# Attention keys projected ahead of values, values handled by halves, and stepped reads in place of stepped writes

## The chip, the cores and the metric

The kernel runs on one core of one Trainium2 chip. Five engines work at the same time, each through its own list of instructions in order: PE multiplies matrices, DVE (the vector engine) and ACT (the scalar engine) work on tiles, POOL does vector work and starts DMAs, SP starts DMAs. Engines wait for each other through semaphores. The metric is the time on the device in microseconds (us), lower is better. A tile lies in SBUF; the results of PE lie in PSUM.

## What is computed

One layer of a decoder trunk over 1024 tokens with 1024 channels, in float32. The input is normalised and projected; three groups of heads mix the tokens; their outputs are joined, projected and added to the stream; a gated MLP with a short convolution and a gated per-layer embedding follow, and a last normalisation.

```python
z = rmsnorm(h, norm_mix_g[l]) @ w_in[l]
a_q, a_f, a_i, a_g, b_q, b_k, b_v, c_in = jnp.split(z, splits, axis=-1)
o_a = hgrn2_mix(a_q, a_f, a_i, a_g, lbs[l], hgrn_gnorm_g[l])
o_b = dilated_window_mix(b_q, b_k, b_v)
o_c, v_first = rwkv7_mix(c_in, ...)
h = h + jnp.concatenate([o_a, o_b.astype(o_a.dtype), o_c.astype(o_a.dtype)], axis=-1) @ w_out[l]
h = h + conv_glu_ffn(rmsnorm(h, norm_ffn_g[l]), ffn_up[l], ffn_conv_w[l], ffn_conv_b[l], ffn_down[l])
gate = jax.nn.sigmoid(rmsnorm(h, norm_ple_g[l]) @ ple_gate[l])
h = h + gate * (p[l] @ ple_proj[l])
return rmsnorm(h, final_norm_g)
```

The change lies in `dilated_window_mix` and in what feeds it. That is a causal attention of four heads of 64 channels, in which each token looks back through three windows at once: the last 128 tokens, the last 512 in steps of 4, and the last 2048 in steps of 16. The first is called near here and the other two far. Tokens whose numbers have the same rest by 4 are a class; the far windows stay within a class.

## The kernel before

**Products in three passes.** Float32 operands are split in a high and a low half, and every large product is made of three matmuls (`mm3`, lines L154, L156, L158). The weight's high half is a cast on ACT (L126). The low half is made in one of two ways that alternate with a running number, `self.uid`: a subtraction on DVE (L132), or a negative copy on ACT and a POOL DMA that adds the weight again (L129, L130).

**Stages.** First the RWKV heads (`rwkv`), with the first projections running beside them as filling. Then `phase_mix` runs five streams in turn, by a list written by hand: `A` and `B` the HGRN heads (`hgrn_head`, two after each other in each stream), `C` the windowed attention (`swa`), `F` the last four projections (`project_late`), `M` what is left of the filling. The lists of the engines follow the order in which these streams issue. Then comes the output projection (L1638 stands on its matmuls and on those of the MLP), the MLP and the embedding.

**Projections into DRAM.** Each of the projected groups of 128 channels, numbered j, goes through a tile `zst` (L556 multiplies by the norm's factor `rstd`) to a DRAM tensor `z`, and is loaded again as `zl` where it is needed (`zload`, L591). Groups 24 to 29 are queries, keys and values of the attention: 24, 25, 26 for the first pair of heads (p=0), 27, 28, 29 for the second (p=1). For these `by_class` turns the two views of L556, so that the tokens of each block of 128 lie by class in `zst`. Groups 24 to 27 are finished in one operation of 128x1024 (source `dp`), 28 and 29 in two halves of 128x512 (source `zp`), each with its own store (L579). The list `js` sets the order of the projections; its last four, here 29, 28, 18, 22, are those of stream `F`.

**The attention.** `swa` runs over the pairs p and, in each, ten steps `qb`. `swa_load` starts the loads of q, k and v on POOL's queue (for p=1 in step 7 of p=0). `swa_values_in` turns v with eight transposes (`vt`, L1267), copies them to `sV` on ACT (L1268), and SP writes them to a DRAM tensor `vd` in four DMAs (L1272). In step 2 `swa_far_values` reads all of `vd` back as `sW` in one DMA (L1276). A step makes scores (`swq`, L1296 near and L1304 far), a masked copy with a running minimum on DVE (`lg`, L1318), the exponential on ACT (L1319), transposes (`swt`, L1335), near values (`swo`, L1350) and, every fourth step, far values (`swf`, L1360, added by L1364). `swa_out` then spreads the reciprocal sums over the channels with 16 matmuls (`swd`, L223) and multiplies (L1373), once for the blocks 0 to 3 and once for the blocks 4 to 7 of a pair, in the step after their far values.

**Beside it** in the rows below: `hsc` (L1121) are scores of an HGRN head, masked on DVE into `hS` (L1123 to L1128); `qt` (L1134) and `hk` (L1132) scale its queries and keys from level to level; L1075 makes `qt` from a loaded q; `hss`, `hrs` and `ho` (L1198, L1201 on POOL, L1203) are its norm; L1405 splits a finished head for the output projection. `Tb` and `Tt` (L783, L785) are the RWKV inverse, a chain of small operations on DVE, whose result goes through two DMAs (`Tz`, `Tc`) to `py` (L896).

Of the kernel before, what the change touches and what calls it, by code (L numbers as in the profile page):

```python
# [10 lines left out]
F32 = mybir.dt.float32  # L11
# [3 lines left out]
ALU = mybir.AluOpType  # L15
# [3 lines left out]
P = 128  # L19
T = 1024  # L20
HT = 512
ND = 8
# [69 lines left out]
class Trunk:  # L92
# [197 lines left out]
    def slot(self, s):  # L290
        return self.slots.tile([P, T], F32, tag="slot", name=self.nm(s), bufs=self.NSLOT)
# [257 lines left out]
    def by_class(self, j, dst, *src):  # L549
        if j < 24:  # L550
            return dst, *src
        return dst.rearrange("p (b c i) -> p b i c", c=4, i=32), *(t.rearrange("p (b i c) -> p b i c", c=4, i=32) for t in src)

    def finish(self, kind, dst, src, r):
        if kind == 2:
# [53 lines left out]
    def rwkv(self):  # L609
        nc, tc = self.nc, self.tc  # L610
        lt = self.mix_in(0, 6, "lora")
        nc.scalar.activation(lt[0:64, :], lt[0:64, :], AF.Tanh)
        sg = self.mix_in(1, 7, "sg")
        nc.scalar.activation(sg, sg, AF.Sigmoid)
        self.z, self.quiet = {}, False
        js = iter((*range(8, 16), 24, 25, 26, 16, 17, 20, 21, 19, 23, 27, 29, 28, 18, 22))
        for p in (0, 1):
            d = {}
            lead, n = self.FILL[p]
            fill = self.project_rest([next(js) for _ in range(n)])  # L620
            with tc.tile_pool(name=f"pre{p}", bufs=1) as tp:
                self.rwkv_prep(p, tp, lt, d, fill)
                self.rwkv_inverse(p, tp, d)
            for i in range(8 * lead - (3 if p else 8)):
                self.quiet = i >= 8 * lead - 20
                next(fill)
                if p == 0 and i == 1:
                    d["v"] = self.mix_in(4, 4, "v")
                if i == (7 if p else 16):
                    self.rwkv_bonus(d)  # L630
            with tc.tile_pool(name=f"rk{p}", bufs=1) as rp:
                self.quiet = False
                self.rwkv_main(p, rp, sg, d, fill)
            self.rwkv_norm(p, sg, d, 1, fill, 6 - 3 * p)
            if p == 0:
                for _ in fill:
                    pass
        self.rest, self.more = list(js), fill
# [259 lines left out]
    def rwkv_group(self, g, rp, d):  # L898
# [9 lines left out]
        def c3(t):  # L908
            return t.rearrange("p (c i) -> p c i", i=64)[:, cs, :]
# [14 lines left out]
        be, kh, v = c3(d["be"]), c3(d["kh"]), c3(d["v"])  # L924
        W, KV = rt("W", [P, 2, 4, 128], 3), rt("KV", [P, 2, 4, 64], 3)
        for srcs, dst in (((a, be), W[:, :, :, 0:64]), ((kh, v), KV)):
            pt = mx("pt", 2, 4, 64)
# [132 lines left out]
    def hgrn_head(self, h):  # L1060
# [52 lines left out]
        for l in range(1, 8):  # L1113
# [30 lines left out]
            yield  # L1144
        V = self.slot("hV")
        for hf in (0, 1):
            pt = mxp.tile([P, HT], F32, tag="mx", name=self.nm("vt"))
            for c in range(4):
                nc.tensor.transpose(pt[:, c * P:(c + 1) * P], vc[:, hf * HT + c * P:hf * HT + (c + 1) * P], self.ident)
            nc.scalar.copy(V[:, hf * HT:(hf + 1) * HT], pt)  # L1150
        kt = self.slot("hkt")
# [12 lines left out]
        for hf in (0, 1):  # L1164
            pk = mxp.tile([P, 4, P], F32, tag="mx", name=self.nm("hkv"))
            for c in range(4):
                cc = hf * 4 + c
                if cc == 7:
                    break
                nc.tensor.matmul(pk[:, c, :], kt[:, at(cc, True)], V[:, at(cc)], start=True, stop=True)  # L1170
            for c in range(4):
# [12 lines left out]
        for hf in (0, 1):  # L1184
            po = mxp.tile([P, 4, P], F32, tag="mx", name=self.nm("hpo"))
            for c in range(4):
                cc = 7 - c if hf == 0 else c
                s = at(cc)
                nc.tensor.matmul(po[:, c, :], S[:, s], V[:, s], start=True, stop=cc == 0)
                if cc:  # L1190
# [36 lines left out]
    def swa(self, sp):  # L1227

        pend, fin, load = [], None, self.swa_load(sp, 0)
        self.nc.gpsimd.dma_start(self.swmask, self.a["swm"])  # L1230
        yield
        for p in (0, 1):
            d = load
            self.swa_values_in(d)
            for qb in range(10):
                if fin:
                    self.swa_out(*fin)
                    fin = None
                if qb == 2:
                    self.swa_far_values(d)  # L1240
                if qb < 8:
                    cur = self.swa_scores(sp, d, qb)
                if qb > 1:
                    fin = self.swa_values(sp, d, *pend.pop(0))
                if 0 < qb < 9:
                    pend[-1:] = [self.swa_turn(sp, *pend[-1])]
                if qb < 8:
                    pend.append((qb, *cur))
                if qb == 7 and p == 0:
                    load = self.swa_load(sp, 1)  # L1250
                yield
        self.swa_out(*fin)

    def swa_load(self, sp, p):
        d = {"p": p}
        for i, n in enumerate("qkv"):
            d[n] = self.zload(24 + 3 * p + i, lambda n: sp.tile([P, T], F32, tag="sslot", name=self.nm(n), bufs=5),
                              self.nc.gpsimd)
        return d

    def swa_values_in(self, d):
        nc, vc = self.nc, d["v"]
        V = self.sp.tile([P, T], F32, tag="sslot", name=self.nm("sV"), bufs=5)
        for hf in (0, 1):
            pt = self.mxp.tile([P, HT], F32, tag="mx", name=self.nm("vt"))
            for c in range(4):
                nc.tensor.transpose(pt[:, c * P:(c + 1) * P], vc[:, hf * HT + c * P:hf * HT + (c + 1) * P], self.ident)  # L1267
            nc.scalar.copy(V[:, hf * HT:(hf + 1) * HT], pt)  # L1268
        d["V"] = V.rearrange("p (b c) -> p b c", c=P)
        d["vd"] = vd = self.zpool.tile([4, ND, 32, P], F32, tag=f"vd{d['p']}", name=f"vd{d['p']}")  # L1270
        for c in range(4):
            nc.sync.dma_start(vd[c].rearrange("b i x -> i b x"), d["V"][32 * c:32 * c + 32])  # L1272

    def swa_far_values(self, d):
        W = self.sp.tile([P, ND, P], F32, tag="sslot", name=self.nm("sW"), bufs=5)
        self.nc.sync.dma_start(W, d["vd"].rearrange("c (g b) i x -> (b i) (c g) x", g=2))  # L1276
        d["W"] = W

    HEADS = slice(0, 64), slice(64, 128)

# [59 lines left out]
    def swa_values(self, sp, d, qb, den, pT):  # L1340
        nc, near = self.nc, pT[0]
        if qb == 0:
            d["o"] = self.sp.tile([P, T], F32, tag="sslot", name=self.nm("ob"), bufs=5) if d["p"] else                 self.keep.tile([P, T], F32, tag="zst", name=self.nm("ob"), bufs=2)
        o = d["o"]
        po = self.mxp.tile([P, P], F32, tag="mx", name=self.nm("swo"))

        blocks = range(max(qb - 1, 0), qb + 1)
        for i, kb in enumerate(blocks):
            for h, hs in enumerate(self.HEADS):
                self.mark = nc.tensor.matmul(po[hs, :], d["V"][:, kb, hs], near[h][:, i * P:(i + 1) * P],  # L1350
                                             start=i == 0, stop=kb == qb).ins
        nc.scalar.copy(o[:, qb * P:(qb + 1) * P].rearrange("p (i c) -> p i c", c=4), po.rearrange("p (c i) -> p i c", c=4))
        if qb % 4 == 3:
            nc.vector.reciprocal(den[:, :8], den[:, :8])
            pf = self.mxp.tile([P, 4, P], F32, tag="mx", name=self.nm("swf"))
            for c in range(4):
                cs = slice(32 * c, 32 * c + 32)
                for g in range(1 + qb // 4):
                    for h, hs in enumerate(self.HEADS):
                        self.mark = nc.tensor.matmul(pf[hs, :, cs], d["W"][:, 2 * c + g, hs],  # L1360
                                                     pT[1][h][:, :, g * P + 32 * c:g * P + 32 * c + 32],
                                                     start=g == 0, stop=g == qb // 4).ins
            on = o[:, (qb - 3) * P:(qb + 1) * P].rearrange("p (b i c) -> p b i c", c=4, i=32)
            nc.vector.tensor_tensor(on, on, pf.rearrange("p b (c i) -> p b i c", c=4), ALU.add)  # L1364
            return d, qb, o, den

    def swa_out(self, d, qb, o, den):
        nc, k = self.nc, 4 + d["p"]
        pd = self.mxp.tile([P, HT], F32, tag="mx", name=self.nm("swd"))
        self.spread2(pd, den, 4)  # L1370
        os = slice((qb - 3) * P, (qb + 1) * P)
        nat = "p (b i c) -> p b i c"
        nc.vector.tensor_tensor(self.final(k, qb == 3, o[:, os]).rearrange(nat, c=4, i=32), o[:, os].rearrange(nat, c=4, i=32),  # L1373
                                pd.rearrange("p (b c i) -> p b i c", c=4, i=32), ALU.mult)
        if qb == 7:
            self.o[k] = o
            self.o_done(k)
# [819 lines left out]
```

## Time and profile before

| | us |
|---|---|
| median of three timed runs | 1393.27 (1393.27 to 1393.94) |
| the profiled execution's own time | 1394.56 |
| span of its instructions | 1392.8 |
| PE busy | 1356.2 (97%) |
| DVE busy | 1059.5 (76%) |
| ACT busy | 648.4 (47%) |
| POOL busy | 350.7 (25%) |

The profile is of one execution. Its times count from the start of the span; the granted clock of PE is given as a share of full speed. In the rows of the timeline the columns are start, duration, engine, line, operation, the tile written and the tiles read, their shapes and the count, and in brackets how long the engine was idle before and what ended that. A start, a plus and a duration give an end. Since matmuls overlap, the time that a group takes from PE is the distance from its start to the next group's start.

### The profile page before, as it was taken

What the parts mean: (1) busy time and instruction counts of PE and PEld (TensorE: products, weight loads), DVE (VectorE), ACT (ScalarE), POOL (GpSimd) and SP (SyncE); (2) the same over time, 40 slices, a digit from 0 to 9 for tenths busy, and PEclk for the clock granted to TensorE, in tenths of its full rate; (3) what the DMA queues carried; (4) which work ended last, traced back from release to release, by engine and by line L of the source; (5) the groups of instructions that cost most, each with busy time, mean ns of one, the idle gap of its engine ahead of it and who ended that gap; (6) DMA issues with size and microseconds to landing.
All of it is one profiled execution on the core that took longest, in us unless ns stands there. A gap on an engine that the chain in (4) does not pass through costs nothing.

```text
span 1392.8 us, 22767 instructions
## 1 busy us (share of the span) xinstructions
PE 1356.2 (97%) x8717; PEld 1101.8 (79%) x8717; DVE 1059.5 (76%) x1689; ACT 648.4 (47%) x1139; POOL 350.7 (25%) x288
## 2 busy tenths in 40 slices
PE   9999999999998999998999999999999999999997
PEld 7878777877876877787888888888888888888886
DVE  7585456835666797789798898888898799677665
ACT  7633433234354464575644434344434445455662
POOL 0211122101321121221254445454543000002321
PEclk9999999999998999999999999999999999999998
DMA  6355533645942311895433233222225963442674
GB/s 233 84 143 146 137 108 91 173 89 142 287 140 99 93 61 62 230 303 177 136 107 106 100 112 113 86 102 101 99 99 190 340 218 106 128 138 68 174 205 136
DMA packets 101757, 197.12 MB, mean 142 GB/s; under 512 B 22160, under 2 KB 28560, under 8 KB 101648
## 3 DMA queue, kind: packets, MB, share of 16 engines
q1 hardware_dynamic: 77040, 157.54, 33.5%
q0 software_dynamic: 13536, 26.86, 10.6%
q10 hardware_dynamic: 11072, 11.28, 2.4%
q8 instruction: 68, 1.11, 0.3%
q14 instruction: 41, 0.34, 0.1%
HBM read 142.42 MB, written 51.64 MB: 139 GB/s over the span
## 4 chain that ended last, share of the span: by engine, by line
PE 84%; DVE 8%; ACT 3%; DMA 2%; issue 1%; POOL 1%; SPq 0%; DVEq 0%; ACTq 0%; POOLq 0%
PE bg L1638 17%; PE bv L1638 13%; PE bv L1965 7%; PE bg L1965 7%; PE dp L154 5%; PE dp L156 5%; PE dp L158 5%; PE dp L1638 3%; PE zo L1638 2%; PE bv L154 1%; PE bv L158 1%; PE bv L156 1%; PE bg L154 1%; PE bg L158 1%; PE bg L156 1%
## 5 line engine op out<-in xcount | busy, mean ns | idle before, releaser
L132 POOL TENSOR_TENSOR wlo<-raw,whi 128x512 fp32r<-128x512 f32 x80 | 128.3, 1622 | 69.7 <-ACT whi L126 69.7
L1638 PE MATMUL bg<-t,whi 128*128 128x512 f32 x352 | 135.0, 395 | 4.6 <-DVE h L1664 4.6
L126 ACT CAST whi<-wraw 128x512 fp32r<-128x512 f32 x120 | 73.6, 618 | 138.6 <-PE dp L156 97.3
L154 PE MATMUL dp<-xh,whi 128*128 128x512 f32 x416 | 136.2, 408 | 0.9 <-DVE r L605 0.8
L158 PE MATMUL dp<-xh,wlo 128*128 128x512 f32 x416 | 130.0, 392 | 0.0
L156 PE MATMUL dp<-xl,whi 128*128 128x512 f32 x416 | 129.3, 391 | 0.1
L126 ACT CAST whi<-raw 128x512 fp32r<-128x512 f32 x88 | 52.4, 620 | 97.7 <-issue 51.2
L1965 PE MATMUL bg<-t,whi 128*128 128x512 f32 x308 | 95.2, 390 | 0.0
L1965 PE MATMUL bv<-t,whi 128*128 128x512 f32 x308 | 94.9, 389 | 0.0
L158 PEld LDWEIGHTS dp<-xh,wlo 128*128 128x128 f32 x416 | 77.9, 188 | 19.2 <-issue 2.0
L156 PEld LDWEIGHTS dp<-xl,whi 128*128 128x128 f32 x416 | 78.2, 188 | 17.4 <-DVE xl L428 0.5
L126 ACT CAST whi<-s 128x512 fp32r<-128x512 f32 x65 | 38.5, 620 | 112.9 <-PE bg L1638 111.0
L132 POOL TENSOR_TENSOR wlo<-s,whi 128x512 fp32r<-128x512 f32 x40 | 59.0, 1475 | 126.1 <-ACT whi L126 126.1
L154 PEld LDWEIGHTS dp<-xh,whi 128*128 128x128 f32 x416 | 74.7, 188 | 20.2 <-issue 5.1
L1638 PEld LDWEIGHTS bg<-t,whi 128*128 128x128 f32 x352 | 67.0, 191 | 19.1 <-DVE h L1664 5.0
L130 POOL DMA_DIRECT2D wlo<-in_w_in_dram x27 | 24.0, 913 | 187.3 <-ACT wlo L129 149.0
L209 POOL TENSOR_TENSOR rst<-rst,mhalf 128x4 f32<-128x4 f32 (+2 forms) x8 | 9.7, 1218 | 243.0 <-DVE rst L205 228.5
L1961 ACT CAST t<-t 128x512 fp32r<-128x512 f32 x77 | 47.8, 622 | 45.6 <-PE bv L1965 32.3
L1638 PE MATMUL bg<-t,wlo 128*128 128x512 f32 x176 | 68.8, 395 | 0.0
L1965 PEld LDWEIGHTS bv<-t,whi 128*128 128x128 f32 x308 | 57.8, 188 | 12.0
L1965 PEld LDWEIGHTS bg<-t,whi 128*128 128x128 f32 x308 | 57.8, 188 | 11.9
L132 DVE TENSOR_TENSOR wlo<-wraw,whi 128x512 fp32r<-128x512 f32 x77 | 52.5, 684 | 18.8 <-ACT whi L126 16.3
(480 smaller groups left out, 3675.7 us busy)
## 6 DMA issues: line engine op xcount, KB each, us to landing
raw<-in_ffn_up_dram SPq DMA_DIRECT2D x44, 512.0 KB, 3.3
wraw<-in_w_in_dram SPq DMA_DIRECT2D x27, 512.0 KB, 4.2
z<-zst SPq DMA_DIRECT2D x18, 512.0 KB, 3.1
gb<-ct SPq DMA_DIRECT2D x33, 256.0 KB, 2.3
t<-gb SPq DMA_DIRECT2D x33, 256.0 KB, 2.7
t<-gt SPq DMA_DIRECT2D x33, 256.0 KB, 2.6
zl<-z SPq DMA_DIRECT2D x16, 512.0 KB, 4.8
wraw<-in_ple_gate_dram SPq DMA_DIRECT2D x16, 512.0 KB, 4.1
```

Source lines behind the costliest of these rows:

```text
L126: self.cast = nc.scalar.copy(hi, src).ins
L130: nc.gpsimd.dma_start(lo, eng, accum_op=ALU.add)
L132: eng.tensor_tensor(lo, src, hi.bitcast(F32), ALU.subtract)
L154: nc.tensor.matmul(ps[hf], wh, xh[hf], start=first, stop=False)
L156: nc.tensor.matmul(ps[hf], wh, xl[hf], start=False, stop=False)
L158: self.step = nc.tensor.matmul(ps[hf], wl, xh[hf], start=False, stop=last).ins
L209: self.pow = nc.gpsimd.tensor_tensor(r2, r, self.mhalf[:, :n], ALU.pow).ins
L1638: self.step = nc.tensor.matmul(ps, w[part == 2][:, s], X[k][part == 1], start=start and k == part == 0, stop=k == 3 and part == 2, skip_gr ...
L1961: nc.scalar.copy(xh, x)
L1965: nc.tensor.matmul(ps[m], wt[part == 2][:, m * P:(m + 1) * P], (xh, xl)[part == 1], start=k == part == 0, stop=k == NK - 1 and part == 2)
```

## The change

It has four parts. First, `by_class` writes `zst` in order and reads `dp`, `zp` and `rstd` in steps of four, where before it read in order and wrote in steps; the contents of `zst` stay the same. Second, the late keys (28) are projected ahead of the late values (29). Third, v comes in two halves: two loads of 256 KB, four transposes and one copy for each, the second half in step 2; `vd` is written in eight DMAs of 64 KB, and `sW` read in two of 256 KB, in steps 2 and 5. Fourth, the last `swa_out` (p=1, blocks 4 to 7) spreads and multiplies in four PSUM tiles of 128 columns.

```diff
     def by_class(self, j, dst, *src):
         if j < 24:
             return dst, *src
-        return dst.rearrange("p (b c i) -> p b i c", c=4, i=32), *(t.rearrange("p (b i c) -> p b i c", c=4, i=32) for t in src)
+        return dst.rearrange("p (b c i) -> p b c i", c=4, i=32), *(t.rearrange("p (b i c) -> p b c i", c=4, i=32) for t in src)
...
-        js = iter((*range(8, 16), 24, 25, 26, 16, 17, 20, 21, 19, 23, 27, 29, 28, 18, 22))
+        js = iter((*range(8, 16), 24, 25, 26, 16, 17, 20, 21, 19, 23, 27, 28, 29, 18, 22))
...
-            self.swa_values_in(d)
+            self.swa_values_in(d, 0)
             for qb in range(10):
...
-                if qb == 2:
-                    self.swa_far_values(d)
+                if qb in (2, 5):
+                    self.swa_far_values(d, qb // 5)
...
+                if qb == 0:
+                    self.swa_load_v(d, 1)
+                if qb == 2:
+                    self.swa_values_in(d, 1)
                 if qb == 7 and p == 0:
                     load = self.swa_load(sp, 1)
...
     def swa_load(self, sp, p):
-        d = {"p": p}
-        for i, n in enumerate("qkv"):
-            d[n] = self.zload(24 + 3 * p + i, lambda n: sp.tile([P, T], F32, tag="sslot", name=self.nm(n), bufs=5),
-                              self.nc.gpsimd)
+        d = {"p": p, "W": {}}
+        slot = lambda n: sp.tile([P, T], F32, tag="sslot", name=self.nm(n), bufs=5)
+        for i, n in enumerate("qk"):
+            d[n] = self.zload(24 + 3 * p + i, slot, self.nc.gpsimd)
+        d["v"], d["V"] = slot("v"), None
+        self.swa_load_v(d, 0)
         return d
...
+    def swa_load_v(self, d, g):
+        gs = slice(g * HT, (g + 1) * HT)
+        self.nc.gpsimd.dma_start(d["v"][:, gs], self.z[26 + 3 * d["p"]][:, gs])
...
+    def swa_values_in(self, d, g):
+        nc = self.nc
+        if g == 0:
+            V = self.sp.tile([P, T], F32, tag="sslot", name=self.nm("sV"), bufs=5)
+            d["V"] = V.rearrange("p (b c) -> p b c", c=P)
+            d["vd"] = self.zpool.tile([2, 4, 4, 32, P], F32, tag=f"vd{d['p']}", name=f"vd{d['p']}")
+        pt = self.mxp.tile([P, 4, P], F32, tag="mx", name=self.nm("vt"))
+        for b in range(4):
+            o = g * HT + b * P
+            nc.tensor.transpose(pt[:, b], d["v"][:, o:o + P], self.ident)
+        V = d["V"][:, 4 * g:4 * g + 4]
+        nc.scalar.copy(V, pt)
         for c in range(4):
-            nc.sync.dma_start(vd[c].rearrange("b i x -> i b x"), d["V"][32 * c:32 * c + 32])
-
-    def swa_far_values(self, d):
-        W = self.sp.tile([P, ND, P], F32, tag="sslot", name=self.nm("sW"), bufs=5)
-        self.nc.sync.dma_start(W, d["vd"].rearrange("c (g b) i x -> (b i) (c g) x", g=2))
-        d["W"] = W
+            nc.sync.dma_start(d["vd"][g, c].rearrange("b i x -> i b x"), V[32 * c:32 * c + 32])
+
+    def swa_far_values(self, d, g):
+        if g == 0:
+            d["W"] = self.sp.tile([P, 2, 4, P], F32, tag="sslot", name=self.nm("sW"), bufs=5)
+        self.nc.sync.dma_start(d["W"][:, g], d["vd"][g].rearrange("c b i x -> (b i) c x"))
...
     def swa_out(self, d, qb, o, den):
         nc, k = self.nc, 4 + d["p"]
-        pd = self.mxp.tile([P, HT], F32, tag="mx", name=self.nm("swd"))
-        self.spread2(pd, den, 4)
         os = slice((qb - 3) * P, (qb + 1) * P)
         nat = "p (b i c) -> p b i c"
-        nc.vector.tensor_tensor(self.final(k, qb == 3, o[:, os]).rearrange(nat, c=4, i=32), o[:, os].rearrange(nat, c=4, i=32),
-                                pd.rearrange("p (b c i) -> p b i c", c=4, i=32), ALU.mult)
+        dst, src = (t.rearrange(nat, c=4, i=32) for t in (self.final(k, qb == 3, o[:, os]), o[:, os]))
+        n = 1 if d["p"] and qb == 7 else 4
+        for b in range(0, 4, n):
+            pd = self.mxp.tile([P, n * P], F32, tag="mx", name=self.nm("swd"))
+            self.spread2(pd, den[:, 2 * b:], n)
+            nc.vector.tensor_tensor(dst[:, b:b + n], src[:, b:b + n], pd.rearrange("p (b c i) -> p b i c", c=4, i=32), ALU.mult)
```

Each name that is given counts `self.uid` up by one, and the change gives names in another number; so the two ways of making a low half change places for the first of the four late weights, and for the weights of the embedding's gate. The far matmuls (L1360) read the same values from `sW`, which now lies half by half. Line numbers shift by up to 15 from L1234 on.

**First place: the attention's second pair is loaded and begun.** On POOL the three loads stand in one place of the program, ahead of an HGRN operation; `zl_4694` is k and `zl_4696` v, and `z_4344` and `z_4033` are the DRAM tensors of groups 28 and 29. Before:

```order
88 L1132 TENSOR_TENSOR hk_4327<-hk_4327,hT_4395 128x2x64x4
89 L591 DMA zl_4694<-z_4344 128x1024
90 L591 DMA zl_4696<-z_4033 128x1024
91 L1132 TENSOR_TENSOR hk_4327<-hk_4327,hT_4395 128x2x16x16
92 L1201 TENSOR_TENSOR hrs_4705<-hss_4702,mhalf 128x8
```

Now, where `zl_4700` is k and `v_4702` v, and `z_4028` (group 28) is the tensor that is projected first, `z_4349` (group 29) the second:

```order
89 L1132 TENSOR_TENSOR hk_4332<-hk_4332,hT_4400 128x2x64x4
90 L591 DMA zl_4700<-z_4028 128x1024
91 L1269 DMA v_4702<-z_4349 128x512 x2
92 L1132 TENSOR_TENSOR hk_4332<-hk_4332,hT_4400 128x2x16x16
93 L1201 TENSOR_TENSOR hrs_4711<-hss_4708,mhalf 128x8
```

The loads keep their place; k now reads the tensor that is finished first, and v the one that is finished second, half by half.

On PE, where that pair's scores begin, `swo_4723` and `swt_4730` of before are the last steps of the first pair, `swq` the first scores of the second. Before:

```order
2106 L1121 MATMUL hsc_4708<-qt_4330,ks_4650 64x64 x8
2107 L1350 MATMUL swo_4723<-pT_4676,sV_3961 64x128
...
2111 L1296 MATMUL swq_4936<-zl_4694,zl_4692 128x128 x2
2112 L1304 MATMUL swq_4936<-zl_4694,zl_4692 32x128 x8
2113 L1335 MATMUL swt_4730<-cst,lg_4664 128x128 x4
...
2117 L1121 MATMUL hsc_4749<-qt_4330,ks_4720 64x64 x8
2118 L154 MATMUL zp_4777<-xh_108,whi_4766 128x512
```

Now:

```order
2106 L1121 MATMUL hsc_4714<-qt_4335,ks_4656 64x64 x8
2107 L1308 MATMUL swq_4936<-zl_4700,zl_4698 128x128 x2
2108 L1316 MATMUL swq_4936<-zl_4700,zl_4698 32x128 x8
2109 L1363 MATMUL swo_4729<-pT_4682,sV_3961 64x128
...
2113 L1347 MATMUL swt_4736<-cst,lg_4670 128x128 x4
...
2117 L1121 MATMUL hsc_4755<-qt_4335,ks_4726 64x64 x8
2118 L154 MATMUL zp_4783<-xh_108,whi_4772 128x512
```

The same matmuls stand between the two `hsc`; the first scores moved ahead of `swo`.

**Second place: some 50 us later.** On DVE the rows run from the norm of an HGRN head to the `L556` of the first half of group 22. Before:

```order
646 L1199 TENSOR_SCALAR hss_5176<-hss_5176 128x8
647 L1132 TENSOR_TENSOR hk_4805<-hk_4805,hT_4864 128x2x8x32
648 L1203 TENSOR_TENSOR ho_5099<-ho_5099,hrs_5179 128x1024
649 L1070 TENSOR_SCALAR zl_5237<-zl_5237,olb,lb 128x1024
650 L1405 TENSOR_TENSOR xh_5478<-oc_1874 128x512
651 L556 TENSOR_TENSOR zst_5193<-zp_5195,rstd 128x512
```

Now:

```order
644 L1199 TENSOR_SCALAR hss_5187<-hss_5187 128x8
645 L1203 TENSOR_TENSOR ho_5100<-ho_5100,hrs_5190 128x1024
...
648 L1132 TENSOR_TENSOR hk_4811<-hk_4811,hT_4870 128x2x8x32
649 L1070 TENSOR_SCALAR zl_5248<-zl_5248,olb,lb 128x1024
650 L1420 TENSOR_TENSOR xh_5489<-oc_1874 128x512
651 L1073 TENSOR_SCALAR hk_5305<-zl_5248 128x512 x2
652 L1367 RECIPROCAL sden_4935<-sden_4935 128x8
653 L1420 TENSOR_TENSOR xh_5491<-oc_3511 128x512
654 L1420 TENSOR_TENSOR xh_5493<-zl_4704 128x512
655 L556 TENSOR_TENSOR zst_5204<-zp_5206,rstd 128x512
```

Two more splits (L1420, L1405 of before), two L1073 and a reciprocal stand ahead of `L556` now, and the `hk` operation behind `ho`.

At the same time SP starts the loads of HGRN head 3 (`z_3459` and `z_3710`, its f and q). Now the second half's four `vd` writes lie between them:

```order
125 L591 DMA zl_5248<-z_3459 128x1024
126 L1284 DMA vd_4914<-sV_4913 32x4x128 x4
127 L591 DMA zl_5250<-z_3710 128x1024
128 L1289 DMA sW_5120<-vd_4914 128x4x128
129 L579 DMA z_5205<-zst_5204 128x512
```

Before, the two loads followed each other, and the four `vd` writes and the `sW` load stood together, four rows further up.

More of the change, by code (lines that the diff above doesn't have):

```diff
@@ L1254, in swa_load @@
     def swa_load(self, sp, p):
-        d = {"p": p}
-        for i, n in enumerate("qkv"):
-            d[n] = self.zload(24 + 3 * p + i, lambda n: sp.tile([P, T], F32, tag="sslot", name=self.nm(n), bufs=5),
-                              self.nc.gpsimd)
-        return d
[L1261 to L1270, printed above, removed]
-        for c in range(4):
-            nc.sync.dma_start(vd[c].rearrange("b i x -> i b x"), d["V"][32 * c:32 * c + 32])
@@ L1342, in swa_values @@
         if qb == 0:
-            d["o"] = self.sp.tile([P, T], F32, tag="sslot", name=self.nm("ob"), bufs=5) if d["p"] else                 self.keep.tile([P, T], F32, tag="zst", name=self.nm("ob"), bufs=2)
+            d["o"] = self.sp.tile([P, T], F32, tag="sslot", name=self.nm("ob"), bufs=5) if d["p"] else \
+                self.keep.tile([P, T], F32, tag="zst", name=self.nm("ob"), bufs=2)
         o = d["o"]
@@ L1359, in swa_values @@
                     for h, hs in enumerate(self.HEADS):
-                        self.mark = nc.tensor.matmul(pf[hs, :, cs], d["W"][:, 2 * c + g, hs],
+                        self.mark = nc.tensor.matmul(pf[hs, :, cs], d["W"][:, g, c, hs],
                                                      pT[1][h][:, :, g * P + 32 * c:g * P + 32 * c + 32],
```

## The prediction

> **What bounds the kernel now.** I read first the busy time by windows (window, length, then busy time and count of each engine, PE's granted clock, DMA share, GB/s).
>
> ```profile
> 400.00:440.00 40.00, 39.53 (x461) 30.88 (x459) 29.00 (x74) 20.94 (x51) 4.91 (x5) 1.00 0.16 45
> 440.00:460.00 20.00, 14.07 (x122) 10.46 (x121) 11.44 (x26) 5.24 (x15) 5.82 (x6) 0.74 0.43 152
> ...
> 480.00:500.00 20.00, 19.02 (x219) 14.40 (x217) 16.56 (x38) 11.48 (x27) 4.48 (x3) 1.00 0.34 119
> 500.00:520.00 20.00, 19.26 (x236) 15.40 (x236) 19.44 (x46) 14.20 (x32) 3.10 (x4) 1.00 0.12 42
> ...
> 700.00:1300.00 600.00, 599.52 (x2652) 496.30 (x2651) 516.48 (x632) 273.51 (x411) 190.42 (x124) 1.00 0.39 131
> ```
>
> PE, third number of a row, is full nearly everywhere: 599.52 of 600 us in the long stage at the end. Time can be won only where PE stands idle, and the one wide hole near this change is 440 to 460, with 14.07 busy at a clock of 0.74. Between 500 and 520 DVE, at 19.44 of 20, is as full as PE. Next come PE's waits (total, times, longest).
>
> ```profile
> PE swq L1296 <- DMA zl<-z: 5.9, 1, 5.9
> ...
> PE swd L223 <- DVE hS L1099: 1.4, 1, 1.4
> PE swt L1335 <- DVE zst L556: 1.0, 1, 1.0
> ...
> PE py L896 <- DMA Tc<-Tz: 1.2, 1, 1.2
> ```
>
> The hole is one wait: the first scores of the second pair stand 5.9 us for a load. The chain of work that ended last says why (start, us, what).
>
> ```profile
> 435.67 1.08 DVE zst L556
> 436.77 2.96 DMA z<-zst
> ...
> 440.36 8.03 DMA zl<-z
> ```
>
> The second half of the keys is scaled, stored, and loaded again, the load alone taking 8.03 us. Two rows of the timeline, of the load and of the store of group 29's second half:
>
> ```profile
> 440.36 1.14 POOL L591 DMA_DIRECT2D zl<-z  x2 [14.33 <-PE swo L1350]
> 402.89 0.32 SPq L579 DMA_DIRECT2D z<-zst  x1
> ```
>
> POOL was idle for 14.33 us before the load, so it was ready from 426.03 on. The row names PE's `swo` as releaser; the program has the load wait for the two stores of the keys and for the scores that last read its buffer, and 436.77 + 2.96 = 439.73 fits the second store's landing. I take the store.
>
> **Key and value order, and the halves.** The keys now take the place of the values in stream `F`, whose second store was issued at 402.89 (the last row above). At 2.96 us a store they lie in DRAM by about 406. The load into k's buffer must still wait for the last scores of the first pair, which end where the `hsc` below begins, at 429.26. So it is issued near 429.3 instead of 440.36, and lands at 429.3 + 8.03 = 437.3. The scores need it near 441.7: 4.4 us of margin. The values' second half, not the keys, now waits for the store of 439.7; its transposes come only after 466, and POOL's queue is held no longer than before.
>
> What PE saves is read in its timeline.
>
> ```profile
> 382.55 0.49 PE L1296 MATMUL swq<-zl,zl 64*128 64x128 f32 x4
> ...
> 383.36 1.15 PE L1095 MATMUL hsc<-zl,hk 128*64 128x64 f32 x32
> ...
> 427.87 0.70 PE L1296 MATMUL swq<-zl,zl 64*128 64x256 f32 x4
> ...
> 429.26 0.70 PE L1121 MATMUL hsc<-qt,ks 128*64 128x64 f32 x16
> 429.89 0.50 PE L154 MATMUL zp<-xh,whi 128*128 128x512 f32 x1
> ...
> 439.97 1.09 PE L1335 MATMUL swt<-cst,lg 128*128 128x128 f32 x8
> 440.99 0.69 PE L1121 MATMUL hsc<-qt,ks 128*64 128x64 f32 x16
> 441.70 0.92 PE L1350 MATMUL swo<-pT,sV 128*64 128x128 f32 x8
> ...
> 449.86 1.97 PE L1335 MATMUL swt<-cst,lg 128*128 128x128 f32 x8
> ...
> 454.57 0.56 PE L154 MATMUL zp<-xh,whi 128*128 128x512 f32 x1
> ```
>
> From the end of `swo` (441.70 + 0.92 = 442.62) to the next projection (454.57) there are 11.95 us: 5.90 of wait and 6.05 of work at a low clock, since the same eight `swt` take 1.97 there against 1.09 at 439.97. At full clock the work is, from one start to the next, 383.36 − 382.55 = 0.81 for the first scores, 1.02 for `swt`, 429.26 − 427.87 = 1.39 for the second scores, and 0.63 for `hsc`: 3.85 in all. With no wait at all 11.95 − 3.85 = 8.1 us would go.
>
> What is late next is on DVE. The `hsc` ahead of the projection reads `qt`, and DVE makes it behind `ho`, which waits for POOL's `hrs`:
>
> ```profile
> 445.16 1.23 DVE L1203 TENSOR_TENSOR ho<-ho,hrs 128x1024 f32<-128x1024 f32 x1 [1.44 <-POOL hrs L1201]
> 446.30 0.68 DVE L1134 TENSOR_TENSOR qt<-qt,hT 128x512 f32<-128x512 f32 x1
> ```
>
> That chain hangs on earlier work of the HGRN head, so it does not move: `qt` ends at 446.98. PE reaches `hsc` at 442.62 + 0.81 + 1.02 + 1.39 = 445.84 and waits 1.1 us. The projection starts at 446.98 + 0.63 = 447.61 instead of 454.57: **−7.0 us**. Behind the waiting `hsc` stands PE's whole list, so this wait is paid in full. I keep −8.1 (no wait) for the range.
>
> **Stepped reads.** The four groups 24 to 27 and the halves of 28 and 29 change their access.
>
> ```profile
> L556 DVE TENSOR_TENSOR zst<-dp,rstd 128x1024 f32<-128x1024 f32 x4 | 8.1, 2020 | 0.0
> L339 DVE TENSOR_TENSOR dp<-dp,rstd 128x1024 f32<-128x1024 f32 x10 | 12.3, 1226 | 13.6 <-PE dp L158 13.6
> L1364 DVE TENSOR_TENSOR ob<-ob,swf 128x512 f32<-128x512 f32 x4 | 2.8, 690 | 0.3
> L1139 DVE TENSOR_TENSOR hT<-zl 128x512 f32<-128x512 f32 x4 | 2.7, 684 | 0.0
> ```
>
> With stepped writes the mean is 2020 ns; the same product read and written in order takes 1226. No row reads `rstd` from SBUF in steps of four numbers, but L1364 reads PSUM in steps of 32 and takes 690 for 512 columns, and L1139 reads SBUF in steps of two and takes 684: steps cost nothing when reading. So I take 1226, 0.8 us less for each of four, with 2020 or more as the other end. Three of them stand in the RWKV inverse, a chain on DVE whose result goes through two DMAs to PE's `py`. The last of them is:
>
> ```profile
> 274.16 2.06 DVE L556 TENSOR_TENSOR zst<-dp,rstd 128x1024 f32<-128x1024 f32 x1
> ```
>
> Three times 0.8 is 2.4 us on the chain, but PE waits there for only 1.2 (`py <- Tc`, quoted above), and then is bound by its own work: **−1.2 us**, and 0 if the reads are slow. The fourth, and the halves (1.08 at 435.67, some 0.69 in order), stand where PE is full (39.53 of 40 us up to 440), and hide under its projections: 0, and a further gain of up to 0.8 + 4 × 0.39 = 2.4 us if PE did wait there.
>
> [...]
>
> **From 461 to 500** DVE is nearly full and its order changes. `swd`, which waited 1.4 us for a masked copy (`hS` L1099), now waits for the far sum that stands ahead of it: −1.4 to 0. L1070 (0.81 in the row below) moves from an idle stretch behind a masked copy: up to +0.8. I take both in full, −0.6, because `swd`'s wait is a row and its new releaser stands several operations earlier.
>
> ```profile
> 490.64 0.69 DVE L1132 TENSOR_TENSOR hk<-hk,hT 128x512 f32<-128x512 f32 x1
> 492.86 1.23 DVE L1203 TENSOR_TENSOR ho<-ho,hrs 128x1024 f32<-128x1024 f32 x1 [1.53 <-POOL hrs L1201]
> 494.00 0.81 DVE L1070 TENSOR_SCALAR zl<-zl,olb,lb 128x1024 f32<-128x1024 f32 x1
> 494.72 0.68 DVE L1405 TENSOR_TENSOR xh<-oc 128x512 f32<-128x512 f32 x1
> ...
> 497.32 0.75 DVE L1073 TENSOR_SCALAR hk<-zl 128x512 f32<-128x512 f32 x2
> 497.99 1.22 DVE L1075 TENSOR_TENSOR qt<-zl,zl 128x1024 f32<-128x1024 f32 x1
> ```
>
> At 494 two more L1405 (0.68 each), L1073 (0.75) and a small reciprocal stand ahead of the `L556` for which `swt` already waits 1.0: up to 2.3 us more of that wait. `hk` (490.64), which filled 0.7 us of the wait for `hrs`, moves behind it: +0.7 of idle DVE. The moved work is missing later, where DVE is full, so the true price lies between 0.7 and 2.3; I take the middle, **+1.5 us**.
>
> **The rest costs 0.** Four more DMA starts (eight `vd` writes for four) and one `sW` load stand on SP, which has gaps of several us; the transposes and copies are the same number. The last multiply in four pieces adds under 1 us of DVE while PE has other HGRN products: between −0.3 and +0.7, taken 0. The changed halves of the gate's weights come from POOL or DVE in a stage where PE waits for neither: ±1, taken 0.
>
> **Sum:** −7.0 − 1.2 − 0.6 + 1.5 = −7.3 us. The profiled execution took 1394.56 on its own clock, 1.3 above the median of 1393.27 and outside the three runs; 1394.56 − 7.3 = 1387.3, and from the median 1386.0. I forecast between them, **1386.6**.
>
> **Rivals.** *All of it comes:* `hsc` meets no wait and DVE loses nothing: −8.1 − 1.2 − 1.4 = −10.7, about 1382.6. For it: DVE's L1139 and L1132 can slide. Against: the wait for `hrs` in two rows above. Chance 0.13.
>
> *DVE is the bound from 455 to 540:* it works 19.44 of 20 us there, so of the 7.0 us gained only what its idle time holds can be kept. Its busy share is 16.56 at 480 to 500, which leaves 3.4 us to take up; then −3.4 − 1.2 = −4.6 at best, and with the +1.5 about −3, near 1390.3. Chance 0.18.
>
> *Stepped reads are slow:* the sum without the 1.2, −6.1, about 1387.8. Chance 0.12.
>
> *Slower: the q load of HGRN head 3 waits behind `vd`.* SP starts its DMAs in order, and the four writes of the second half wait for transposes and ACT's copy. Before, both loads were issued together (first row; the second is the writes, the third the median from issue to landing of SP's loads from 380 to 560):
>
> ```profile
> 486.43 0.79 SPq L591 DMA_DIRECT2D zl<-z  x2
> 467.37 1.86 SPq L1272 DMA_DIRECT2D vd<-sV  x4
> ...
> zl<-z SPq DMA_DIRECT2D x11, 512.0 KB, 3.9
> ```
>
> Now q follows the second half's `swt` (about 487.2), transposes 0.6, a copy 0.6 and 1.86 of issue: 490.2. It lands 3.9 to 8.0 us later, between 494.1 and 498.2 on before's clock; L1075 wants it at 497.99. Each us later stops DVE's whole list. To be slower than before by 2.8 us it must land some 10 us late, at 508; that needs the copy at about 498, behind a stalled exponential on ACT, say. Chance 0.06; at that point, 1393.27 + 2.8 = 1396.1.
>
> *The change doesn't do what it says:* if PE's `swo` really released the loads at 440.36, as the row says, k lands when it did, and only the −1.2 is left: 1392.1. Chance 0.05.
>
> **How the numbers follow.** The forecast holds 0.46, 1384 to 1389.5. Some 0.2% of this time, 2.8 us, is about what a measurement of this kernel can tell from no change. The range from 1382 to 1392 holds all but the slower case, the top of the fifth and some of the tails. Faster by over 2.8: forecast, first and third rival, and 0.10 of the second: 0.81; within: the other 0.08 and 0.05, 0.13; slower 0.06.
>
> **What would show it.** In the profile after, `swq`'s wait for `zl` is gone; the clock of 440 to 460 is 1.00; a wait of about 1 us of `hsc` for `qt` stands near 446; `zst` 128x1024 takes about 1.23 us; `py` waits for nothing; `swt` waits up to 3 us for `L556` near 487. The prediction is wrong if k's load still starts after 438, if `zst` stays at 2 us, or if DVE waits for `zl` at L1075.

## The result and the profile after

The changed kernel takes 1383.59 us (median of four runs, 1381.94 to 1383.71) against 1393.27 for the kernel before (1391.38 to 1393.94). The ratio is 0.993, with a 95% interval of 0.9913 to 0.9947. The time lies in the predicted range of 1382 to 1392, 3 us below the predicted value and just under the 1384 to 1389.5 that the prediction gave to its own account; the gain did not come from where the prediction put it.

The busy time by windows of the kernel after, columns as in the prediction:

```profile
400.00:440.00 40.00, 39.53 (x461) 30.95 (x459) 29.24 (x73) 20.82 (x51) 6.06 (x7) 1.00 0.23 70
440.00:460.00 20.00, 18.00 (x232) 14.65 (x230) 15.58 (x33) 6.85 (x18) 6.06 (x5) 0.91 0.42 154
...
600.00:700.00 100.00, 100.00 (x454) 82.85 (x453) 91.47 (x136) 65.07 (x104) 28.39 (x26) 1.00 0.64 192
```

The hole from 440 to 460 is down from 6 us to 2, but its clock is 0.91. The last row is the surprise: in the window from 600 to 700, where the change has no operation, PE is now busy all the time. Before, it was not:

```profile
600.00:700.00 100.00, 95.42 (x421) 78.44 (x420) 83.63 (x131) 63.27 (x103) 22.93 (x22) 0.97 0.65 190
```

PE's waits in the kernel after (line, releaser, total, times, longest):

```profile
PE hsc L1121 <- DVE qt L1134: 3.1, 2, 2.0
PE swt L1347 <- DVE zst L556: 2.5, 1, 2.5
```

The wait for the load is gone; the first scores and their load now read so in the timelines of PE and POOL:

```profile
429.70 0.59 POOL L591 DMA_DIRECT2D zl<-z  x1 [3.52 <-PE swq L1316]
440.49 0.54 POOL L1269 DMA_DIRECT2D v<-z  x1 [9.65 <-DMA z<-zst]
441.75 0.49 PE L1308 MATMUL swq<-zl,zl 64*128 64x128 f32 x4
444.83 0.45 PE L1316 MATMUL swq<-zl,zl 64*32 64x128 f32 x16
447.28 0.69 PE L1121 MATMUL hsc<-qt,ks 128*64 128x64 f32 x16 [2.00 <-DVE qt L1134]
447.89 0.50 PE L154 MATMUL zp<-xh,whi 128*128 128x512 f32 x1
455.10 1.03 PE L1211 MATMUL vt<-cst,ho 128*128 128x128 f32 x8
```

The keys' load is issued at 429.70, as soon as the old scores have been read, the values' second half waits for the store at 440.49, and `swq` follows without a wait. The list of waits before had a line of the MLP that has no counterpart after; this is that matmul, in the timelines of before and after:

```profile
646.98 1.22 PE L1638 MATMUL bg<-t,whi 128*128 128x512 f32 x2 [4.58 <-DVE h L1664]
```

```profile
638.35 0.61 PE L158 MATMUL dp<-peh,pel 128*128 128x512 f32 x2
638.80 0.62 PE L1653 MATMUL bg<-t,whi 128*128 128x512 f32 x2
```

**Where the time went,** by starts of the same PE groups in the two profiled executions. At `hsc` before `swo` after is 0.15 behind (440.99 and 441.14). The projection starts at 447.89 against 454.57: 6.7 ahead. The `vt` behind that projection starts at 455.10 against 460.21: 5.1 ahead. The output projection (`zo`) starts at 556.96 against 560.39: 3.4 ahead. The first `bg` of the MLP starts at 638.80 against 646.98, 8.2 ahead, and from 663 on every group is 11.0 ahead, to the end (spans 1381.8 and 1392.8). So 3.4 us of the 11.0 come from the stage that was changed, and 7.6 from the start of the MLP: 4.8 up to the first `bg`, nearly all of it the 4.6 of idle PE, and 2.8 behind it, where PE's clock before stood at 0.50 for the 5 us from 646.98 on.

### The profile page after: what moved, and what is told of

It reads as the page before. It is cut to its first block, busy times and chain, and to the rows that moved or that the text cites. A ratio compares the mean times of both kernels' runs of the same rounds, so it can differ in the third digit from the quotient of the medians.

```text
span 1381.8 us, 22800 instructions
## 1 busy us (share of the span) xinstructions
PE 1353.7 (98%) x8717; PEld 1099.5 (80%) x8717; DVE 1067.9 (77%) x1692; ACT 649.1 (47%) x1139; POOL 352.3 (25%) x290
## 4 chain that ended last, share of the span: by engine, by line
PE 86%; DVE 7%; issue 2%; ACT 2%; POOL 1%; DMA 1%; SPq 0%; DVEq 0%; ACTq 0%; POOLq 0%
PE bg L1653 17%; PE bv L1653 13%; PE bv L1980 8%; PE bg L1980 8%; PE dp L154 6%; PE dp L158 5%; PE dp L156 5%; PE dp L1653 2%; PE zo L1653 2%; PE bv L154 1%; PE bv L158 1%; PE bv L156 1%; PE bg L154 1%; PE bg L158 1%; PE bg L156 1%
## 5 line engine op out<-in xcount | busy, mean ns | idle before, releaser
L132 DVE TENSOR_TENSOR wlo<-wraw,whi 128x512 fp32r<-128x512 f32 x77 | 56.0, 730 | 27.4 <-ACT whi L126 18.9
```

What stands on the lines that cost most here:

```text
L132: eng.tensor_tensor(lo, src, hi.bitcast(F32), ALU.subtract)
```

## The experiments

**Why the MLP's start no longer waits.** The order of PE and DVE there is the same before and after. L1664 (L1679 after) multiplies the MLP's input by its norm, eight times for each half of the tokens, and reads the norm's factor from a PSUM tile `ps_ss` of that half. What differs is the semaphore value that the first `bg` matmul waits for: in the kernel before it is the last L1664 of the second half; after, the last L1679 of the first half. The first `bg` tile takes two PSUM banks, 4 and 5, that the pool `mx` had used before, and `ps_ss` is an `mx` tile. The eight L1664 of the second half in DVE's timeline before, then the eight L1679 after, and the second `bg` tile of PE after:

```profile
641.57 5.35 DVE L1664 SCALAR_TENSOR_TENSOR h<-h,par,ps_ss 128x512 f32<-128x512 f32 x8
```

```profile
638.14 5.35 DVE L1679 SCALAR_TENSOR_TENSOR h<-h,par,ps_ss 128x512 f32<-128x512 f32 x8
644.24 0.62 PE L1653 MATMUL bg<-t,whi 128*128 128x512 f32 x2
```

Before, the first `bg` (646.98) stands until the eight end at 646.92. After, it starts at 638.80 while they still run. There `ps_ss` is in bank 6, and it is the second `bg` tile, in banks 6 and 7, that waits for them in the program; it starts at 644.24, when they have ended (643.49), and PE does not stop. The built programs place the tile that L1664 reads so:

```
kernel                               second half's ps_ss   first bg waits for
before                               bank 5                last L1664 of the second half
after                                bank 6                last L1679 of the first half
before, keys first                   bank 7                an earlier operation
before, keys first, four pieces      bank 4                last of the second half
after, two pieces                    bank 5                last of the second half
after, three pieces                  bank 7                an earlier operation
before, four pieces                  bank 7                last of the first half
after, old key order                 bank 6                an earlier operation
before, keys first, halves           bank 4                last of the second half
before, keys first, two pieces, F    bank 7                last of the first half
```

(`F` stands for the order of stream `F` in the last experiment.) So the theory: the stop depends on the bank into which `mx` happens to rotate, which an added, removed or reordered `mx` tile can move. The rival: cutting the last multiply lets the tail end sooner. Five kernels were made to tell them apart.

*Keys first alone* (on the kernel before):

```diff
-        js = iter((*range(8, 16), 24, 25, 26, 16, 17, 20, 21, 19, 23, 27, 29, 28, 18, 22))
+        js = iter((*range(8, 16), 24, 25, 26, 16, 17, 20, 21, 19, 23, 27, 28, 29, 18, 22))
```

> The kernel before with only the late keys projected ahead of the late values (all else of before). Theory (PSUM bank): the stop of the first bg matmul before 647 depends only on the PSUM bank that the second half's ps_ss tile falls into; in this build that tile is in bank 7, outside bg's banks 4 and 5, so PE does not wait for h there, though no multiply is cut in four. Expected: wait of bg for DVE h gone (0 against 4.6 us), and the span from the zo start at 560 on to 660 shorter by 7.6 us; with the load of the keys no longer waited for, 3 to 7 us more, in all 1379 to 1383 us against 1393.3. Rival (the four pieces): the stop goes only with the cut multiply, so here it stays at 4.6 us, and the time is 1386 to 1390.

Measured 1379.61 us against 1393.03 (ratio 0.9898, 0.9883 to 0.9913). One edit of the four gives more than all of them. There is no wait of `bg` for h, with an uncut multiply, and the first `bg` follows at 636.66. From 441 to `zo` PE gains 5.9 us (5.57 ahead at `zo`, 0.32 behind at 441), against 3.6 with the full change.

*Keys first and four pieces* (the new `swa_out` as in the change):

> The kernel before with the late keys first and the last multiply in four PSUM tiles; v whole and stepped writes as before. Theory (PSUM bank): here the second half's ps_ss tile falls into bank 4, inside bg's banks, so bg waits 4 to 5 us for DVE h although the multiply is cut: 1386 to 1390 us. Rival (the four pieces): no such wait, 1379 to 1383 us.

1386.74 us (0.9953, 0.9941 to 0.9966), with this line among PE's waits:

```profile
PE bg L1640 <- DVE h L1666: 4.6, 1, 4.6
```

The multiply is cut and the stop is there, as the bank says. The gain from 441 to `zo` is 5.7, so the four pieces cost PE 0.25 us (at `swd` 6.46 ahead of before, at the next `hkv` 6.21).

*Two pieces, and three, in the changed kernel:*

```diff
-        n = 1 if d["p"] and qb == 7 else 4
+        n = 2 if d["p"] and qb == 7 else 4
```

> The changed kernel with the last multiply in two PSUM tiles of 256 columns in place of four. Theory (PSUM bank): ps_ss of the second half is in bank 5, inside bg's banks: the wait of bg for DVE h of 4 to 5 us is back and with the slow clock behind it 7 to 8 us, 1391 us against 1383.6. Rival (pieces free the tail sooner): two pieces lose at most a few tenths, 1383 to 1385 us, no wait of bg.

1388.89 us (0.9972, 0.9963 to 0.9982), 2 below the expected 1391 and well above the rival's 1385, and in the list of waits:

```profile
PE bg L1653 <- DVE h L1679: 4.6, 1, 4.6
```

```diff
-        n = 1 if d["p"] and qb == 7 else 4
-        for b in range(0, 4, n):
+        for b, n in ((0, 2), (2, 1), (3, 1)) if d["p"] and qb == 7 else ((0, 4),):
```

> The changed kernel with the last multiply in three PSUM tiles (256, 128 and 128 columns). Theory (PSUM bank): ps_ss of the second half is in bank 7, outside bg's banks: no wait of bg, 1383.6 us within 1. Rival (number of pieces): between the two pieces and the four.

1381.96 us (0.9919, 0.9905 to 0.9932), 1.6 below the 1383.6 where 1 was allowed, and no wait of `bg`. Two pieces have the stop, three and four have not: beside those 0.25 us the number of pieces matters only through the bank.

*Four pieces alone on the kernel before:*

> The kernel before with only the last multiply in four PSUM tiles. Theory (PSUM bank): ps_ss of the second half is in bank 7, outside bg's banks: the wait of bg for h (4.6 us) and the clock of 0.5 behind it go, 7.6 us in all, and nothing else changes beside 0.3 us at swd: swq still waits 5 to 7 us for the load; 1393.0 - 7.4 = 1385.6. Rival (the late stop goes because the mix ends earlier): no change, 1393.

1386.44 us against 1392.52 (0.9957, 0.9941 to 0.9973). The stop of `bg` is gone while `swq` still waits 5.3 us for its load. The gain of 6.1 is somewhat under the 7.4 expected; the ranges of the runs (1384.8 to 1388.1 and 1390.7 to 1396.7) are wide. The price of the stop itself differs between executions: with the same wait of 4.6 the clock stood at 0.50 for 6.8 us in the profile of the kernel before, 1.1 of them still in the wait, and for 3.4 in that of keys first and four pieces. The wait of `bg` was as the bank theory says in all five, and as the rival says in none that tells them apart.

**Key order undone in the changed kernel.**

```diff
-        js = iter((*range(8, 16), 24, 25, 26, 16, 17, 20, 21, 19, 23, 27, 28, 29, 18, 22))
+        js = iter((*range(8, 16), 24, 25, 26, 16, 17, 20, 21, 19, 23, 27, 29, 28, 18, 22))
```

> The changed kernel with the late values projected ahead of the late keys again; the second half's ps_ss is in bank 6, so no wait of bg. Theory: swq waits 5 to 7 us for the load of the keys and PE loses what it had gained there, 5 us with the clock: 1388 to 1390 us. Rival (the halves alone let the load land in time): 1384.

1388.21 us (0.9966, 0.9954 to 0.9978), 4.6 above the changed kernel. `swq` waits 5.1 us for its load again, with the halves in place: the halves do not bring the keys sooner, the order does. From 441 to `zo` PE even loses 1.8 us against the kernel before (0.2 ahead to 1.6 behind); what this kernel still gains comes behind `zo`, where `bg` does not stop.

**Stepped reads.** In three of the groups the product or the factor is read in order. It is to show whether the step costs where the factor `rstd` is read, in SBUF (then groups 25 and 27 are slow), or as one of two rivals has it; the times are those of one operation of 128x1024 in us:

```diff
+        st, ct = "p (b i c) -> p b c i", "p (b c i) -> p b c i"
+        v = lambda t, r: t.rearrange(r, c=4, i=32)
+        if j == 24:
+            return v(dst, ct), v(src[0], st), v(src[1], ct)
+        if j == 25:
+            return v(dst, ct), v(src[0], ct), v(src[1], st)
+        if j == 26:
+            return v(dst, ct), v(src[0], ct), v(src[1], ct)
```

> The changed kernel in which L556 takes its factor or its product in natural order for three groups: group 24 reads only the product from PSUM in steps of four (factor in order), group 25 reads only the factor rstd from SBUF in steps of four (product in order), group 26 reads both in order; group 27 stays as in the changed kernel, both stepped. So tokens of groups 24 to 26 get the factor of another token or lie in natural order, and the output is not the reference's. [...] Rival (the step costs on the side of PSUM): 2.0 for 24 and 27, 1.23 for 25 and 26. Second rival (any stepped operand halves the rate): 2.0 for 24, 25 and 27.

The four operations in DVE's timeline, of groups 24, 25, 26 and 27 in this order:

```profile
250.11 1.22 DVE L564 TENSOR_TENSOR zst<-dp,rstd 128x1024 f32<-128x1024 f32 x1
262.04 1.96 DVE L564 TENSOR_TENSOR zst<-dp,rstd 128x1024 f32<-128x1024 f32 x1
273.80 1.21 DVE L564 TENSOR_TENSOR zst<-dp,rstd 128x1024 f32<-128x1024 f32 x1
382.13 2.03 DVE L564 TENSOR_TENSOR zst<-dp,rstd 128x1024 f32<-128x1024 f32 x1
```

A step of four float32 read from PSUM cost nothing (1.22 against 1.21 in order), the same step read from SBUF cost 0.75 us (1.96). The price lies on the side of SBUF: groups 25 and 27 are slow, and neither the 24 and 27 of the first rival nor the 24, 25 and 27 of the second. The whole kernel took 1382.97 us in its one run, 0.6 under the changed kernel.

*Stepped writes put back in the changed kernel* (`by_class` as before):

> The changed kernel with the stepped writes of before in place of stepped reads; the PSUM banks are the same as in the changed kernel. Theory (steps cost the same on either side): 128x1024 of L556 2.02 us against 1.98, time 1383.6 within 0.8, py waits 0 to 0.5 us. Rival (the prediction's term): py waits 1.2 us again and the time is 1384.8.

1383.66 us against 1383.59 for the changed kernel, ratios of 0.9934 (0.992 to 0.9947) and 0.993: this part of the change is worth nothing that these runs can tell. `py` waited 2.3 us in the one profile, more than either theory allows. The two DMAs ahead of it vary between executions: from the start of `Tz` to the main group of `py` it is 8.5 us in the profile of the kernel before, 7.5 in that of the changed kernel and 10.1 here, so I do not read that wait as an effect of the edit.

**The halves** (on the kernel before with keys first):

> The kernel before with keys first and v in halves (one multiply, stepped writes as before). The second half's ps_ss is in bank 4, so the wait of bg for h of 4.6 us is expected. Theory (the halves' reordering of DVE and the later transposes cost 2.3 us between 455 and 556): against the kernel before, PE is 3.6 us ahead at the start of zo, and swt waits 2.5 us for zst; 1388 to 1389 us. Rival (the 2.3 belongs to stepped reads or to the four pieces): 5.6 us ahead at zo, swt waits 1.0, 1386 to 1387.

1390.37 us (0.9983, 0.9972 to 0.9994), against 1379.61 without the halves; but 4.6 us and more of this is the stop of `bg`, which the halves brought back by moving `ps_ss` to bank 4. The theory was only partly right. `swt` waits the expected 2.5 us for `zst`, but PE is 2.2 us ahead at `zo` and not 3.6, and only 0.9 of that was gained since 441: in this execution the clock fell to 0.50 behind that wait as well.

**The clock behind short waits.** So the changed kernel was run twice more.

> The changed kernel again, for the clock behind its waits of 2.0 us (hsc for qt, near 447) and 2.5 us (swt for zst, near 494). Theory (whether the clock drops after such a wait is not fixed by the program): in this and the next run of the same kernel the projection behind the first wait takes 5.6 us in one execution and about 7.2 in another, and the transposes behind the second 1.1 or about 2.0. Rival (it is fixed): 7.2 and 1.1 each time, as in the profile of the changed kernel.

> The same kernel and the same two readings as in the run before: by the theory one of them may differ between the executions, by the rival none does.

They took 1386.45 and 1381.66 us. The `vt` behind the two waits, in the timelines of the first and the second of these runs; the rows are the `vt` behind the projection and the `vt` behind `swt`:

```profile
447.24 0.69 PE L1121 MATMUL hsc<-qt,ks 128*64 128x64 f32 x16 [2.00 <-DVE qt L1134]
455.03 1.03 PE L1211 MATMUL vt<-cst,ho 128*128 128x128 f32 x8
...
497.89 1.97 PE L1211 MATMUL vt<-cst,ho 128*128 128x128 f32 x8
```

```profile
445.28 0.69 PE L1121 MATMUL hsc<-qt,ks 128*64 128x64 f32 x16 [2.00 <-DVE qt L1134]
451.51 1.03 PE L1211 MATMUL vt<-cst,ho 128*128 128x128 f32 x8
...
493.06 1.97 PE L1211 MATMUL vt<-cst,ho 128*128 128x128 f32 x8
```

From the `hsc` to the first `vt` it is 7.8 us in one and 6.2 in the other, for the same matmuls behind the same wait of 2.00; the second `vt` takes 1.97 in both, where it took 1.09 in the profile of the result. So the clock's fall after such a wait is not fixed by the program, and the rival falls. Where it fell and where it did not is read from the traces in the last section.

**A version without the wait.** Keys first on the kernel before, the last multiply in two pieces (bank 7), and stream `F`'s step of round 13 issued ahead of `A` and `B`:

```diff
-                order += "C" * (r in self.TURNS) + "A" + "B" * (r > 5) + "F" * (r in self.LATE)
+                late = "F" * (r in self.LATE)
+                order += "C" * (r in self.TURNS) + late * (r == 13) + "A" + "B" * (r > 5) + late * (r != 13)
```

> The kernel before with keys first, the last multiply in two tiles (ps_ss of the second half in bank 7, outside bg's banks), and stream F's step of round 13 issued ahead of A and B, so that the projection stands ahead of the hsc that waits for qt. Theory (that wait costs its 2.0 us and, by the clock of 0.5 behind it, 1.6 more): no wait of hsc for qt near 446, a clock of 1.00 from 440 to 455, and 3 to 4 us less than with keys first alone (1379.6): 1376. Rival (DVE is full from 455 to 540 and takes it back): PE is ahead at 455 but not at 556, 1379 to 1380 us.

1377.49 us against 1392.17 (0.9893, 0.988 to 0.9907), the fastest of all. Its window:

```profile
436.00:456.00 20.00, 19.54 (x275) 16.35 (x274) 15.39 (x32) 7.61 (x18) 5.69 (x7) 1.00 0.52 185
```

The projection fills the wait (0.46 us of it stay, at 451), the clock stays at 1.00, and from 441 to `zo` PE gains 9.1 us (10.39 ahead, 1.27 of it already at 441), 3.2 more than with keys first alone. DVE did not take it back. In the medians it is 2.1 under keys first alone (1379.61), where 3 to 4 were expected, and 6 under the changed kernel.

## Why the prediction was right, and where it was not

**The load of the keys: right.** The projection was to start 7.0 us sooner with a new wait of `hsc` for `qt`; it starts 6.7 sooner (6.8 against its neighbours at 441), and `qt` decides its start as foreseen. The wait is 2.0 and not 1.1 mainly because PE arrives sooner: I had priced the second scores by a step with 256 far columns (1.39), and here, with 128, they take 1.08; and `hsc` and `swo` ahead of the wait, which I had counted as 1.63 to the end of `swo`, take 1.23 from start to start.

**The clock behind that wait: missed.** I charged the wait its own length. Behind it the projection took 7.2 us instead of 5.6, so 1.6 more were lost in the profiled execution. The clock of 1.00 that I named as a sign was 0.91.

**Stepped reads, −1.2: wrong.** L556 takes 1983 ns on the mean (1.96 to 2.03) instead of 1226, the value of 2 us that the prediction named as a sign of being wrong:

```profile
L556 DVE TENSOR_TENSOR zst<-dp,rstd 128x1024 f32<-128x1024 f32 x4 | 7.9, 1983 | 0.0
```

The step that failed is "steps cost nothing when reading", drawn from a row that steps through PSUM and one that steps by two in SBUF; the third rival, that stepped reads are slow, was the right one. `py` starts at 288.87 against 288.74. Its wait fell to 0.3 in this profile, but not by L556: from the first of the three L556 to the start of `Tz` it is 30.5 us in both profiles, and the two DMAs behind took 7.5 instead of 8.5.

**From 461 to 500, +0.9: too small.** The wait of `swt` grew from 1.0 to 2.5, the 1.5 that I took. But `swd`'s gain was taken back by `vt` waits, and from `vt` at 455 to `zo` PE lost 1.7 (5.1 ahead to 3.4). The kernel with keys first alone gains 0.6 in the same stretch (5.0 ahead to 5.6): of the 2.3 us between them the four pieces have 0.25; the other 2.0 I put down to the halves, with the clock at 1.00 in both, since the changed kernel with the stepped writes loses the same 1.7 there. That is what is left over and not shown by the run of the halves, in which the clock fell. The rival of the q load behind `vd` did not come: DVE shows no wait for a load there.

**"The rest costs 0": wrong by 7.6 us.** I priced the pieces by their own multiplies and took the MLP's wait of 4.6, which the prediction does not mention, as a given, since no instruction moved there. The order of the instructions was unchanged; the tile's bank was not. This one term made up what the others lacked: −6.7 + 1.6 + 1.7 − 7.6 = −11.0, the difference of the spans, where I had summed −7.3. In the medians the gain is 9.7. That the total came out near was luck: the other terms together fell 3.9 us short of the sum, and a term that was not foreseen gave 7.6.

## What to carry to other kernels

When a kernel that rotates PSUM buffers is edited, look at what the first matmul of each later pool waits for: one tile more, fewer or in another place of a rotation can add or remove a stop 100 us later (here of 4.6 us; in the kernel before the last `swd` starts at 546.7, `bg` at 646.98), and the built program shows it before any run. Time each part of a change alone; here one line gave 13.4 us by itself, some 7.5 of them by its bank, more than the four edits together. A wait on the busiest engine should be filled, not only shortened, since its clock may fall behind it, as here to 0.50 behind waits of 2.0 and 2.5 us.

## What the hardware showed beside this

PE's granted clock fell to 0.50 after waits of only 2.0 and 2.5 us, and in some executions only: of ten profiles with the 2.0 wait the clock of the 5 us behind it was 0.66 in seven and 1.00 in three; of nine with the 2.5 wait it was 0.50 to 0.68 in five and 1.00 in four. The two need not go together (the profile of the result has the first only, the second of the two runs above the second only).

The traces show where it fell. Between the start and the end of the program the clock was low for 10.24 and for 6.83 us in the profile of the kernel before and twice for 3.41 in that of the result, which is three, two and one times 3.413. The two falls lie 201.39 us apart in the first of these, 59 times 3.413, and 395.95 in the second, 116 times. This step is called a beat here. Four windows of the first of the two runs above, cut at it, with the 2.0 wait in the first and most of the 2.5 wait in the third:

```profile
445.34:448.75 3.41, 1.51 (x20) 1.34 (x21) 3.21 (x6) 0.00 (x0) 0.80 (x1) 1.00 0.29 113
448.75:452.16 3.41, 3.41 (x10) 2.63 (x9) 3.41 (x7) 0.62 (x1) 1.00 (x1) 0.50 0.00 0
489.71:493.12 3.41, 1.61 (x28) 1.19 (x27) 3.41 (x8) 1.16 (x3) 1.39 (x1) 1.00 0.11 34
493.12:499.95 6.83, 6.14 (x49) 3.90 (x51) 5.62 (x13) 1.75 (x4) 0.00 (x0) 0.50 0.10 40
```

From 448.75 to 493.12 it is 13 times 3.41. There the 2.0 wait lies almost whole in one beat (1.90). In other executions the beat lies elsewhere in the program: in the second of the two runs one ends at 444.19 and cuts the same wait into 0.91 and 1.09. In seventeen of the nineteen cases the timelines tell where the beat lay (the two of the kernel with two pieces, with a clock of 1.00 behind both waits, do not): the clock fell at the end of a beat that held 1.66 us or more of the wait, and did not fall where the beat cut the wait so that neither part was over 1.59. This is read off afterwards; no run moved a wait on purpose, and the limit is not the same everywhere: of the 1.8 us wait of `vt` for `ho` in the profile of the kernel before 1.75 lay in the beat from 557.13 to 560.55, and the clock did not fall at its end.

Of the 4.8 us between the two single runs of the changed kernel (1386.45 and 1381.66) 2.0 were there at the `hsc` at 441.10 and 439.14, and 2.7 came between it and `zo` (559.78 and 555.08). There the clock was low for 10.24 us in the first run, as the windows above have it, and for 3.41 in the second.
